# First group of a two-layer decoder trunk: x turned without its row scale, loads on two queues, another order of casts and products

## The chip, the cores and the metric

One core of one Trainium2 chip runs the whole program, the other cores are idle. The metric is the device time of one execution in microseconds (us), as the median of the runs. The engines are named as in the profile: PE (TensorE, matrix products; PEld is its loading of the stationary operand), DVE (VectorE), ACT (ScalarE), POOL (GpSimd), SP (SyncE, which only issues DMA transfers here). ACT can issue DMA transfers too; a row marked SPq or POOLq is such an issue on that engine.

## What is computed

The reference is a trunk of two layers on x of 256 tokens by 1024 features, in float32. Each layer is a SwiGLU block, a mixer (causal pooling in layer 0, dilated attention in layer 1) and a second SwiGLU block, each with an RMS norm ahead of it and one behind it. The change touches only the very first step:

```python
def rms_norm(x, gain):
    y = x * rsqrt(mean(x * x) + eps) * gain

def swiglu(h, w_gate, w_up, w_down):
    return (silu(h @ w_gate) * (h @ w_up)) @ w_down

f = swiglu(rms_norm(x, g[0]), ffn_w_gate[0, 0], ffn_w_up[0, 0], ffn_w_down[0, 0])
```

The factor rsqrt(...) of a row can be applied after the product with the weights, because it is one number per token. The kernel does so: x times the gain goes into the product, and the row factor comes in at the silu and at the product of gate and up.

## The kernel before

Tokens lie in two tiles of 128 rows (i = 0, 1). Every float32 product is made of three products in a shorter format (float32r): each operand is split into a high part (a cast on ACT) and a low part (the original less the high part, on DVE), and PE adds high times high, high times low, low times high. So every block of weights that arrives must pass ACT once and DVE once before PE can use all of it. PE is fed by a stream of weight blocks, `ws`, in the order of their use; a block is 128 x 2048 floats (1 MB), loaded as two halves of 512 KB into one of three buffers `raw` (or two buffers `xy`).

The first group of the first SwiGLU is `opening()` (L635 to L801). It is 512 columns of gate and 512 of up for both token tiles: 8 pieces of weights j = 0 to 7 (gate 0 to 3, up 4 to 7; block b holds pieces 2b and 2b + 1), each used in 6 products for each tile i, which makes 96 products of 128 x 128 by 128 x 512. Pieces 0, 1, 4 and 5 meet the first 512 features of x, pieces 2, 3, 6 and 7 the second 512.

x must be turned (features on partitions) before it can be the stationary operand. For each tile i and half b: `turn_x` (L667) transposes four 128 x 128 pieces on PE; `scaled_x` (L673) multiplies by the gain on DVE; `high_x` (L681) casts on ACT; `low_x` (L684) subtracts on DVE. Ahead of that the kernel before scales each row by the reciprocal of the largest magnitude of its first 128 elements (`size_x`, `rows`, L647 to L660: a reduce, a maximum, a reciprocal and a multiplication on DVE for the first half of a row; a multiplication on ACT for the second), and `q0` puts that size back later. `high(j)` (L687) and `low(j)` (L696) split piece j of the weights; `products(i, j, ...)` (L700) issues the products H (high weights, high x), W (low weights) and X (low x). `keep_warm` (L86) issues small products of zeros while nothing else is there to do.

Inside `manual_schedule` (L708 to L791) the order of the lines is the order of the instructions on PE, DVE, ACT and SP; each of these engines works through its own queue in order and waits at an instruction whose operands are not there. After that block, Tile's scheduler sets the order. What follows: the mean squares of x (`rstd_of`, four squares L203 on ACT, a power on POOL), differences of the turned halves of x (`Sums`, casts L285, subtractions L286), and `pair(1)` (L378), the second group. In it `form` (L124) splits a whole block at once: hl_hi on ACT (L127, 128 x 2048), hl_lo on DVE (L128). The first formed block feeds the 24 products g; a block in buffer xy the 12 products st that follow; then y is added to x on DVE (L376, `add(x, y, 0)`), the sum is formed and used; another block feeds 24 products g; then a third block z is added to x (L376 again), and the sum is formed for the next st products.

Of the kernel before, what the change touches and what calls it, by code (L numbers as in the profile page):

```python
# [11 lines left out]
F32 = mybir.dt.float32  # L12
# [7 lines left out]
P = 128  # L20
# [9 lines left out]
Q_TAIL = 4  # L30
TURN_0, TURN_1 = 3, 0
DMA_SUMS = (2, 3)
WARM = 26
FILL = 9, 5, 8, 4
LEAST = 1e-3
SIZE_OF = 128
EPS = 1e-6
MAGIC = 12582912.0
SIN_MAX = 3.1415925
# [14 lines left out]
def trunk_kernel(ctx: ExitStack, tc: tile.TileContext, x, pos, gains, pscale, ws, wq, invf, amask, pmat, icnt, out):  # L54
# [37 lines left out]
    nc.sync.dma_start(gfirst[0:KC, 0:P], gains[0].rearrange("(k p) -> k p", p=P))  # L92

    block_no = [0]
    last = {}
# [532 lines left out]
            waiting.append(rest)  # L628

    rx = cp.tile([P, 2], F32, name="r_x")  # L630
    q0 = cp.tile([P, 2], F32, name="q_x")
    aT = new_aT("x")
    sums = Sums("x")

    def opening():  # L635


        gcol = cp.tile([P, KC], F32, name="gain_col")
        size = cp.tile([P, 2], F32, name="size_x")
        over = cp.tile([P, 2], F32, name="over_x")  # L640
        raws, highs, units, t, tps = [], [], [], {}, {}
        banks = [accp.tile([P, 512], F32, tag="acc", name=f"acc_b0{k}") for k in range(4)]
        gu = [banks[0::2], banks[1::2]]
        y = [sc4.tile([P, D], F32, tag="y", name=f"n_x{i}") for i in range(2)]
        H, X, W = [(0, 0, 0), (0, 1, 0)], [(1, 0, 0), (1, 1, 0)], [(0, 0, 1), (0, 1, 1)]

        def size_x(i):  # L647
            z = slice(i, i + 1)
            nc.vector.tensor_reduce(
                size[:, z], h[i][:, :SIZE_OF], axis=mybir.AxisListType.X, op=ALU.max, apply_absolute_value=True  # L650
            )
            nc.vector.tensor_scalar(size[:, z], size[:, z], LEAST, None, op0=ALU.max)
            nc.vector.reciprocal(over[:, z], size[:, z])

        def rows(i, b):
            c, z = slice(b * 512, (b + 1) * 512), slice(i, i + 1)
            if b == 0:
                nc.vector.tensor_scalar_mul(y[i][:, c], h[i][:, c], over[:, z])
            else:
                nc.scalar.mul(y[i][:, c], h[i][:, c], over[:, z])  # L660

        def turn_gain():
            tp = tpp.tile([P, 4, P], F32, tag="tp", name="tp_gain")
            nc.tensor.transpose(tp[:, 0, :KC], gfirst[:KC, :P], ident[:KC, :KC])
            nc.scalar.copy(gcol, tp[:, 0, :KC])

        def turn_x(i, b):  # L667
            tps[i, b] = tp = tpp.tile([P, 4, P], F32, tag="tp", name=f"tp_x{i}{b}")
            for c in range(4):
                k = b * 4 + c  # L670
                nc.tensor.transpose(tp[:, c], y[i][:, k * P : (k + 1) * P], ident)

        def scaled_x(i, b):  # L673
            t[i, b] = sums.tmp(f"{i}{b}")
# [6 lines left out]
        def high_x(i, b):  # L681
            nc.scalar.copy(part_of(i, b)[:, 0], t[i, b])
# [3 lines left out]

        def high(j, k=None):  # L687

            if j == len(highs):
                pool, tag = (xyp, "xy") if j < 2 else (hlp, "hl")  # L690
                highs.append(pool.tile([P, 2, 1024], F32R, tag=tag, name="hl"))
                units.append((highs[j][:, 0], highs[j][:, 1]))
            c = slice(0, 1024) if k is None else slice(k * 512, (k + 1) * 512)
            nc.scalar.copy(highs[j][:, 0, c], raws[j // 2][:, j % 2, c])

# [12 lines left out]
        with tc.manual_schedule(  # L708
            engines={
                mybir.EngineType.PE,  # L710
                mybir.EngineType.DVE,
                mybir.EngineType.Activation,
                mybir.EngineType.SP,
            }
        ):
            nc.sync.dma_start(h[1][:, :512], x[P:, :512])
            raw = rawp.tile([P, 2, 1024], F32, tag="raw", name="raw0")
            for k in range(2):
                c = slice(k * 512, (k + 1) * 512)
                nc.sync.dma_start(raw[:, 0, c], ws[0, :, c])  # L720
            raws.append(load_raw(raw=raw, at=1))
            for i in range(2):
                nc.sync.dma_start(h[i][:, 512:], x[i * P : (i + 1) * P, 512:])
            raws.extend(load_raw() for _ in range(2))
            turn_gain()
            keep_warm(FILL[0])
            size_x(0)
            rows(0, 0)
            turn_x(0, 0)
            size_x(1)  # L730
            rows(1, 0)
            scaled_x(0, 0)
            keep_warm(FILL[1])
            turn_x(1, 0)
            scaled_x(1, 0)
            keep_warm(FILL[2])
            high(0, 0)
            high_x(0, 0)
            high(0, 1)
            low(0, 0)  # L740
            products(0, 0, H)
            low_x(0, 0)
            keep_warm(FILL[3])
            high_x(1, 0)
            products(1, 0, H[:1])
            products(0, 0, W[:1], X)
            low(0, 1)
            products(1, 0, H[1:], W[:1])
            products(0, 0, W[1:])
            products(1, 0, W[1:])  # L750
            low_x(1, 0)
            high(1)
            rows(0, 1)
            rows(1, 1)
            low(1)
            products(1, 0, X)
            turn_x(0, 1)
            for i in range(2):
                products(i, 1, H, X)
            turn_x(1, 1)  # L760
            for i in range(2):
                products(i, 1, W)
            high(2)
            scaled_x(0, 1)
            high_x(0, 1)
            scaled_x(1, 1)
            high_x(1, 1)
            low_x(0, 1)
            products(0, 2, H, X)
            low(2)  # L770
            raws.append(load_raw())
            products(1, 2, H)
            high(3)
            low_x(1, 1)
            products(0, 2, W)
            products(1, 2, W, X)
            low(3)
            for i in range(2):
                products(i, 3, H, X)
            for i in range(2):  # L780
                products(i, 3, W)
            for j in range(4, 8):
                high(j)
                low(j)
                if j == 5:
                    for i in range(2):
                        rstd_of(h_halves(i), f"x{i}", rx[:, i : i + 1])
                        nc.gpsimd.tensor_mul(q0[:, i : i + 1], rx[:, i : i + 1], size[:, i : i + 1])
            for i in range(2):
                for j in range(4, 8):  # L790
                    products(i, j, H, X, W)  # L791
        s3 = sums.tmp("s")
        nc.vector.tensor_sub(s3, t[0, 0], t[1, 0])
        sums.parts(2, s3)
# [557 lines left out]
```

## Time and profile before

| what | us |
| --- | --- |
| median of 3 runs | 944.83 (943.65 to 946.33) |
| profiled execution, its own time | 945.04 |
| its span in the trace | 943.3 |
| PE busy in the span | 930.7 |
| DVE busy | 744.8 |
| ACT busy | 565.6 |

In the rows of the timeline the first number is the start in us from the span's start, the second the length; in brackets stands how long the engine was idle ahead of it and what it waited for. In the rows of the chain of waits the same two numbers stand ahead of the engine, the output's name and the line.

### The profile page before, as it was taken

How to read it: one execution, taken by the hardware profiler on the slowest of the kernel's cores; microseconds unless marked ns; L12 is line 12 of the kernel's file. 1: busy time of each engine (PE TensorE's matmuls, PEld its weight loads, DVE VectorE, ACT ScalarE, POOL GpSimd, SP SyncE). 2: the span in 40 equal slices, each digit the busy share in tenths (PEclk: the TensorE clock that was granted, in tenths of full speed). 3: DMA queues.
4: the chain of work that ended last, by engine and by line, in shares of the span. 5: the costliest groups of instructions: out<-in, count | busy, mean ns of one | idle time of the engine just before them, and what ended most of it. 6: DMA issues, size and time to landing. Idle time of an engine off the chain costs nothing.

```text
span 943.3 us, 12011 instructions
## 1 busy us (share of the span) xinstructions
PE 930.7 (99%) x4513; PEld 767.7 (81%) x4513; DVE 744.8 (79%) x822; ACT 565.6 (60%) x692; POOL 42.7 (5%) x66
## 2 busy tenths in 40 slices
PE   9999999999999999999999999999999999999997
PEld 7878888778888888888888888888898778788885
DVE  7888897889877889878888874686287788888964
ACT  6675665556647576567657653554356776576652
POOL 1000000000100000001000000110000010000000
PEclk9999999999999999999999999999999999999999
DMA  8785976765568698675696865375333546969561
GB/s 328 245 261 191 330 250 183 266 227 198 175 197 257 217 296 265 195 252 190 163 335 145 320 238 207 139 237 168 132 101 135 179 167 166 334 135 379 148 209 44
DMA packets 56777, 202.92 MB, mean 215 GB/s; under 512 B 7496, under 2 KB 7504, under 8 KB 53904
## 3 DMA queue, kind: packets, MB, share of 16 engines
q1 hardware_dynamic: 53472, 178.83, 52.9%
q0 software_dynamic: 3248, 23.33, 12.9%
q8 instruction: 35, 0.57, 0.2%
q14 instruction: 22, 0.18, 0.1%
HBM read 178.02 MB, written 1.05 MB: 190 GB/s over the span
## 4 chain that ended last, share of the span: by engine, by line
PE 86%; DVE 5%; ACT 3%; issue 3%; DMA 2%; POOL 0%; SPq 0%; DVEq 0%; POOLq 0%; ACTq 0%
PE st L354 13%; PE g L150 12%; PE acc_d L484 12%; PE acc_b L150 8%; PE u L150 7%; PE acc_d L150 4%; PE qp L150 4%; PE kp L150 3%; PE q L354 3%; PE vp L150 3%; PE acc_w L150 2%; PE acc_d L354 2%; PE acc_u L150 2%; PE htp L333 2%; DMA raw<-in_ws 1%
## 5 line engine op out<-in xcount | busy, mean ns | idle before, releaser
L110 ACT CAST hl<-raw 128x1024 fp32r<-128x1024 f32 x140 | 145.5, 1051 | 96.3 <-PE acc_d L150 21.9
L111 DVE TENSOR_TENSOR hl<-raw,hl 128x1024 fp32r<-128x1024 f32 x140 | 169.3, 1220 | 38.2 <-ACT hl L110 37.1
L128 DVE TENSOR_TENSOR hl_lo<-xy,hl_hi 128x2048 fp32r<-128x2048 f32 x55 | 125.9, 2289 | 62.2 <-ACT hl_hi L127 62.2
L127 ACT CAST hl_hi<-xy 128x2048 fp32r<-128x2048 f32 x55 | 105.2, 1913 | 67.2 <-PE u L150 24.7
L484 PE MATMUL acc_d<-hl,h 128*128 128x512 f32 x576 | 136.8, 392 | 0.0
L128 DVE TENSOR_TENSOR hl_lo<-raw,hl_hi 128x2048 fp32r<-128x2048 f32 x54 | 123.4, 2286 | 15.2 <-ACT hl_hi L127 15.2
L484 PEld LDWEIGHTS acc_d<-hl,h 128*128 128x128 f32 x576 | 107.2, 188 | 23.4 <-DVE acc_d L543 0.9
L127 ACT CAST hl_hi<-raw 128x2048 fp32r<-128x2048 f32 x54 | 103.3, 1913 | 22.9 <-PE st L354 8.9
L335 ACT CAST h<-htp 128x512 fp32r<-128x512 f32 (+1 forms) x48 | 26.4, 550 | 38.0 <-PE htp L333 38.0
L150 PE MATMUL acc_b<-hl,aT_m 128*128 128x512 f32 x192 | 44.9, 392 | 0.7 <-ACT aT_m L243 0.7
L150 PE MATMUL acc_d<-hl,h 128*128 128x512 f32 x192 | 44.6, 392 | 0.0
L150 PEld LDWEIGHTS acc_b<-hl,aT_m 128*128 128x128 f32 x192 | 35.7, 188 | 8.5 <-ACT aT_m L243 1.2
L150 PE MATMUL g<-hl_hi,aT_m 128*128 128x512 f32 x128 | 42.0, 394 | 0.0
L354 PE MATMUL st<-hl_hi,S_m 128*128 128x512 f32 x128 | 41.9, 393 | 0.0
L150 PE MATMUL u<-hl_hi,aT_m 128*128 128x512 f32 x128 | 41.8, 393 | 0.0
L150 PEld LDWEIGHTS acc_d<-hl,h 128*128 128x128 f32 x192 | 35.7, 188 | 7.3
L374 POOL DMA_DIRECT2D xy<-raw x22 | 19.2, 872 | 445.9 <-DVE hl_lo L128 160.6
L150 PE MATMUL qp<-hl,aT_f 128*128 128x384 f32 x192 | 37.3, 343 | 0.0
L150 PE MATMUL kp<-hl,aT_hk 128*128 128x512 f32 x144 | 34.5, 394 | 0.0
L150 PEld LDWEIGHTS qp<-hl,aT_f 128*128 128x128 f32 x192 | 32.9, 188 | 1.3 <-issue 0.9
L336 DVE TENSOR_TENSOR h<-htp,h 128x512 fp32r<-128x512 f32 (+1 forms) x48 | 30.7, 640 | 4.0 <-ACT h L335 3.6
L150 PE MATMUL vp<-hl,aT_hk 128*128 128x512 f32 x144 | 33.1, 390 | 0.0
(316 smaller groups left out, 1848.9 us busy)
## 6 DMA issues: line engine op xcount, KB each, us to landing
raw<-in_ws SPq DMA_DIRECT2D x265, 512.0 KB, 5.1
xy<-in_ws SPq DMA_DIRECT2D x44, 512.0 KB, 7.4
xy<-raw POOLq DMA_DIRECT2D x22, 1024.0 KB, 8.2
rawq<-in_wq SPq DMA_DIRECT2D x8, 768.0 KB, 4.7
gain_post<-in_gains SPq DMA_DIRECT2D x14, 256.0 KB, 7.1
gain_pre<-in_gains SPq DMA_DIRECT2D x10, 256.0 KB, 7.4
h<-in_x SPq DMA_DIRECT2D x4, 256.0 KB, 5.3
rawpm<-in_pmat SPq DMA_DIRECT2D x2, 512.0 KB, 4.6
```

The source lines that it names most:

```text
L110: nc.scalar.copy(hl[:, 0, :n], raw[:, k, :n])
L111: last["dve"] = nc.vector.tensor_sub(hl[:, 1, :n], raw[:, k, :n], hl[:, 0, :n])
L127: nc.scalar.copy(hi, raw)
L128: last["dve"] = nc.vector.tensor_sub(lo, raw, hi)
L150: last["mm"] = nc.tensor.matmul(o, l, r, start=start, stop=stop)
L333: nc.tensor.transpose(tp[:, k], prod[c, i][:, k * P : (k + 1) * P], ident)
L335: nc.scalar.copy(d[:, 0], tp[:, :nt])
L336: nc.vector.tensor_sub(d[:, 1], tp[:, :nt], d[:, 0])
L354: nc.tensor.matmul(ps, a(z, k), u[v], start=start and k == 0 and n == 0, stop=k == 3 and n == 2, skip_group_check=not start,)
L374: nc.gpsimd.dma_start(dst, src, accum_op=ALU.add)
L484: nc.tensor.matmul(f[i][k], d[:, z], u[v][:, r], start=c == 0 and m == 0, stop=m == 2 and (own is not None or c == NF - 1), skip_group_che ...
```

## The change

- `size_x`, `rows`, `size`, `over`, `q0` and the tiles `y` are gone. `turn_x` transposes h, that is x itself; the row factor `rx` is used where `q0` was.
- The gain and the first half of tile 1 of x are loaded from ACT's queue instead of SP's. Piece 0 of the weights (two transfers of 256 KB) stays on SP and follows the first half of tile 0. Piece 1 (512 KB) is issued from ACT, in ACT's order behind the copy of the gain.
- SP then loads block 2 (pieces 4 and 5), the second halves of x, block 1, and later block 3.
- The pieces are split and used in the order 0, 1, 4, 5, 2, 3, 6, 7 instead of 0 to 7. The second halves of x are turned after the products of piece 1 (tile 0) and after the products H and X of piece 4 (tile 1); before, after those of piece 0 and within those of piece 1.
- All eight pieces are cast ahead of the four squares; before, pieces 6 and 7 came behind them.
- `keep_warm` fills: 28, then 14, 2, 2, instead of 26, then 9, 5, 8, 4.

```diff
-WARM = 26
-FILL = 9, 5, 8, 4
+WARM = 28
+FILL = 14, 2, 2
...
-    nc.sync.dma_start(gfirst[0:KC, 0:P], gains[0].rearrange("(k p) -> k p", p=P))
+    nc.scalar.dma_start(gfirst[0:KC, 0:P], gains[0].rearrange("(k p) -> k p", p=P))
...
+        def load(b):
+            raws[b] = rawp.tile([P, 2, 1024], F32, tag="raw", name=f"raw{b}")
+            for k in range(2):
+                last["dma"] = nc.sync.dma_start(raws[b][:, k], ws[b, :, k * 1024 : (k + 1) * 1024])
...
-                nc.tensor.transpose(tp[:, c], y[i][:, k * P : (k + 1) * P], ident)
+                nc.tensor.transpose(tp[:, c], h[i][:, k * P : (k + 1) * P], ident)
...
-            nc.sync.dma_start(h[1][:, :512], x[P:, :512])
+            nc.scalar.dma_start(h[1][:, :512], x[P:, :512])
...
+            turn_gain()
+            nc.scalar.dma_start(flat[:, 1024:], ws[0, :, 1024:2048])
+            load(2)
             for i in range(2):
                 nc.sync.dma_start(h[i][:, 512:], x[i * P : (i + 1) * P, 512:])
+            load(1)
             turn_x(0, 0)
...
+            load(3)
+            turn_x(0, 1)
+            scaled_x(0, 1)
+            high_x(0, 1)
+            high(5)
+            low_x(0, 1)
+            low(5)
+            for i in range(2):
+                products(i, 4, H, X)
             turn_x(1, 1)
...
-    ffn(0, aT, sums, go, q=q0)
+    ffn(0, aT, sums, go, q=rx)
```

What this makes of the order of the instructions is shown at three places. The first is the front of ACT's queue. raw_174 and raw_171 are the buffer of pieces 0 and 1, raw_180 that of pieces 2 and 3 in the kernel before, raw_178 that of pieces 4 and 5 in the changed one; tp_gain is the turned gain, aT_x the turned x, sum_x x times the gain. The kernel before:

```order
L665 COPY gain_col<-tp_gain 128x8
L694 CAST hl<-raw_174 128x512
L682 CAST aT_x<-sum_x_211 128x4x128
L694 CAST hl<-raw_174 128x512
L682 CAST aT_x<-sum_x_223 128x4x128
L694 CAST hl<-raw_174 128x1024
L660 ACTIVATE n_x_169<-h_100,over_x 128x512
L660 ACTIVATE n_x_170<-h_101,over_x 128x512
L694 CAST hl<-raw_180 128x1024
L682 CAST aT_x<-sum_x_287 128x4x128
L682 CAST aT_x<-sum_x_290 128x4x128
```

The same place in the changed kernel:

```order
L649 COPY gain_col<-tp_gain 128x8
L705 DMA raw_171<-in_ws 128x1024
L677 CAST hl<-raw_171 128x512
L666 CAST aT_x<-sum_x_191 128x4x128
L666 CAST aT_x<-sum_x_198 128x4x128
L677 CAST hl<-raw_171 128x512
L677 CAST hl<-raw_171 128x1024
L677 CAST hl<-raw_178 128x1024
L666 CAST aT_x<-sum_x_265 128x4x128
L677 CAST hl<-raw_178 128x1024
L666 CAST aT_x<-sum_x_289 128x4x128
```

A DMA issue now stands ahead of the first cast. It waits for a semaphore: the semaphores of the transfers are used in turn, and the one of this transfer is that of the first transfer of piece 0, which must have landed. The casts of the second halves of x (the last aT_x rows) stand behind casts of pieces 4 and 5.

The second place is ACT's queue from the last casts of the opening to the first formed block. jk_x are the squares, S_x the casts of the differences, s the silu, raw_428 and raw_405 the first formed block. The kernel before:

```order
L203 ACTIVATE jk_x_333,ss_x_332<-h_100 128x512
L203 ACTIVATE jk_x_335,ss_x_332<-h_100 128x512
L203 ACTIVATE jk_x_342,ss_x_341<-h_101 128x512
L203 ACTIVATE jk_x_344,ss_x_341<-h_101 128x512
L694 CAST hl<-raw_299 128x1024 x2
L285 CAST S_x<-sum_xs 128x512
L285 CAST S_x<-sum_x_223 128x512
L285 CAST S_x<-sum_x_211 128x512
L317 ACT_TABLE_LOAD
L317 ACTIVATE s_0_418<-acc_b_165,q_x 128x512
L127 CAST hl_hi<-raw_428 128x2048
```

The changed kernel:

```order
L677 CAST hl<-raw_257 128x1024 x2
L201 ACTIVATE jk_x_318,ss_x_317<-h_100 128x512
L283 CAST S_x<-sum_xs 128x512
L201 ACTIVATE jk_x_320,ss_x_317<-h_100 128x512
L283 CAST S_x<-sum_x_198 128x512
L201 ACTIVATE jk_x_326,ss_x_325<-h_101 128x512
L315 ACT_TABLE_LOAD
L315 ACTIVATE s_0_395<-acc_b_164,r_x 128x512
L201 ACTIVATE jk_x_328,ss_x_325<-h_101 128x512
L283 CAST S_x<-sum_x_191 128x512
L125 CAST hl_hi<-raw_405 128x2048
```

The same instructions stand ahead of the first formed block: two casts of the last pieces, four squares, three casts of differences, the table load and one silu. Only their order among themselves is another.

The third place is DVE's queue from the first formed block to the second add. xy_466 and xy_443 are the buffer x of `pair(1)`, h the turned result of the first group, m the product of gate and up. The kernel before:

```order
L128 TENSOR_TENSOR hl_lo<-raw_428,hl_hi 128x2048
L286 TENSOR_TENSOR S_x<-sum_x_287,S_x 128x512
L128 TENSOR_TENSOR hl_lo<-xy_466,hl_hi 128x2048
L325 SCALAR_TENSOR_TENSOR m_0_424<-acc_b_168,q_x,s_0_422 128x512
L376 TENSOR_TENSOR xy_466<-xy_466,xy_469 128x2048
L336 TENSOR_TENSOR h_0_0_155<-htp_00_447,h_0_0_155 128x4x128
L128 TENSOR_TENSOR hl_lo<-xy_466,hl_hi 128x2048
L128 TENSOR_TENSOR hl_lo<-raw_521,hl_hi 128x2048
L336 TENSOR_TENSOR h_0_0_155<-htp_01_491,h_0_0_155 128x4x128
L376 TENSOR_TENSOR xy_466<-xy_466,raw_498 128x2048
```

The changed kernel:

```order
L126 TENSOR_TENSOR hl_lo<-raw_405,hl_hi 128x2048
L284 TENSOR_TENSOR S_x<-sum_x_265,S_x 128x512
L323 SCALAR_TENSOR_TENSOR m_0_401<-acc_b_167,r_x,s_0_399 128x512
L126 TENSOR_TENSOR hl_lo<-xy_443,hl_hi 128x2048
L334 TENSOR_TENSOR h_0_0_156<-htp_00_424,h_0_0_156 128x4x128
L374 TENSOR_TENSOR xy_443<-xy_443,xy_446 128x2048
L126 TENSOR_TENSOR hl_lo<-xy_443,hl_hi 128x2048
L334 TENSOR_TENSOR h_0_0_156<-htp_01_468,h_0_0_156 128x4x128
L126 TENSOR_TENSOR hl_lo<-raw_498,hl_hi 128x2048
L374 TENSOR_TENSOR xy_443<-xy_443,raw_475 128x2048
```

These are the same ten instructions. The first h row, which needs transposes by PE and a copy by ACT, has moved from behind the first add to ahead of it.

More of the change, by code (lines that the diff above doesn't have):

```diff
@@ L687, in high @@
         def high(j, k=None):
[L689 removed]
+            if j not in highs:
                 pool, tag = (xyp, "xy") if j < 2 else (hlp, "hl")
[L691 to L692 removed]
+                highs[j] = pool.tile([P, 2, 1024], F32R, tag=tag, name="hl")
             c = slice(0, 1024) if k is None else slice(k * 512, (k + 1) * 512)
@@ L715, in opening @@
         ):
-            nc.sync.dma_start(h[1][:, :512], x[P:, :512])
[L717 to L721, printed above, removed]
+            nc.scalar.dma_start(h[1][:, :512], x[P:, :512])
+            raws[0] = rawp.tile([P, 2, 1024], F32, tag="raw", name="raw0")
+            flat = raws[0].rearrange("p k n -> p (k n)")
@@ L722, in opening @@
+            for c in (slice(0, 512), slice(512, 1024)):
+                nc.sync.dma_start(flat[:, c], ws[0, :, c])
+            turn_gain()
+            nc.scalar.dma_start(flat[:, 1024:], ws[0, :, 1024:2048])
+            load(2)
             for i in range(2):
                 nc.sync.dma_start(h[i][:, 512:], x[i * P : (i + 1) * P, 512:])
[L724 to L728, printed above, removed]
+            load(1)
@@ L729, in opening @@
             turn_x(0, 0)
-            size_x(1)
-            rows(1, 0)
             scaled_x(0, 0)
-            keep_warm(FILL[1])
             turn_x(1, 0)
             scaled_x(1, 0)
-            keep_warm(FILL[2])
+            keep_warm(FILL[0])
             high(0, 0)
             high_x(0, 0)
-            high(0, 1)
[L740 to L746, printed above, removed]
@@ L747, in opening @@
-            low(0, 1)
-            products(1, 0, H[1:], W[:1])
+            low(0, 0)
+            low_x(0, 0)
+            products(0, 0, H[:1])
+            keep_warm(FILL[1])
+            high_x(1, 0)
+            products(0, 0, W[:1])
+            products(1, 0, H[:1], W[:1])
+            products(0, 0, X[:1])
+            keep_warm(FILL[2])
+            high(0, 1)
+            low_x(1, 0)
+            low(0, 1)
+            products(0, 0, H[1:])
+            products(1, 0, H[1:])
+            high(1)
@@ L749, in opening @@
+            products(0, 0, X[1:])
+            products(1, 0, X)
+            low(1)
             products(0, 0, W[1:])
             products(1, 0, W[1:])
[L751 to L757, printed above, removed]
+            high(4)
+            low(4)
             for i in range(2):
                 products(i, 1, H, X)
+            for i in range(2):
+                products(i, 1, W)
@@ L760, in opening @@
+            load(3)
[5 more added lines that the diff above has]
+            low(5)
+            for i in range(2):
+                products(i, 4, H, X)
             turn_x(1, 1)
             for i in range(2):
[L762 to L765, printed above, removed]
+                products(i, 4, W)
             scaled_x(1, 1)
             high_x(1, 1)
-            low_x(0, 1)
@@ L769, in opening @@
[L769 to L773, printed above, removed]
-            low_x(1, 1)
[L775 to L782, printed above, removed]
+            low_x(1, 1)
+            for j in (2, 3, 6, 7):
                 high(j)
@@ L784, in opening @@
                 low(j)
[L785 to L788, printed above, removed]
             for i in range(2):
-                for j in range(4, 8):
+                products(i, 5, H, X, W)
+            for i in range(2):
+                rstd_of(h_halves(i), f"x{i}", rx[:, i : i + 1])
+            for i in range(2):
+                for j in (2, 3):
@@ L791, in opening @@
                     products(i, j, H, X, W)
+            for i in range(2):
+                for j in (6, 7):
+                    products(i, j, H, X, W)
+            block_no[0] = 4
         s3 = sums.tmp("s")
```

23 lines of the change are left out of this document (2 added, 21 removed).

## The prediction

> **What bounds the kernel now.** I first read the busy times of the page and then the chain of waits over the first 60 us, because the change touches only the first group.
>
> ```profile
> span 943.3 us, 12011 instructions
> PE 930.7 (99%) x4513; PEld 767.7 (81%) x4513; DVE 744.8 (79%) x822; ACT 565.6 (60%) x692; POOL 42.7 (5%) x66
> ```
>
> PE is busy for 99% of the span, so a microsecond by which PE's queue is later at 60 us is a microsecond at the end, and one that it gains there is gained at the end. What decides when PE gets to 60 us is another question. The chain of waits from 14 to 50 us, in order of time:
>
> ```profile
> 14.43 0.70 DVE sum_x L676
> 15.15 0.62 ACT aT_x L682
> 15.77 2.85 ACT hl L694 x3
> 18.62 0.63 ACT jk_x L203 x2
> ...
> 26.97 1.81 ACT hl_hi L127
> ...
> 28.80 1.13 DVE hl_lo L128
> ...
> 43.98 2.21 DVE xy L376
> ...
> 48.02 1.92 ACT hl_hi L127
> 49.98 0.49 PE st L354
> ```
>
> There is no PE in it between 14.43 and 49.98. The path starts at the turned second half of x (aT_x), goes through everything that ACT has queued up to the first formed block, and on through DVE and ACT until PE waits for them at 50 us. PE's waits there:
>
> ```profile
> 49.98 0.19 PEld L354 LDWEIGHTS st<-hl_hi,S_x 128*128 128x128 f32 x1 [0.67 <-ACT hl_hi L127]
> 50.50 0.19 PEld L354 LDWEIGHTS st<-hl_lo,S_x 128*128 128x128 f32 x1 [0.33 <-DVE hl_lo L128]
> ```
>
> So up to 50 us the cover that PE's products give to ACT and DVE is used up. If ACT and DVE get there later, PE stops for the difference; if only PE gets there earlier, it waits longer. I therefore follow ACT's queue, and PE only where ACT waits for it.
>
> **The change part by part.** The start of the opening on ACT, DVE, PE and SP:
>
> ```profile
> 0.74 0.39 SPq L74 DMA_DIRECT2D h<-in_x  x1
> 1.19 0.36 SPq L92 DMA_DIRECT2D gain_first<-in_gains  x1
> 2.01 0.90 SPq L720 DMA_DIRECT2D raw<-in_ws  x2
> 2.95 0.43 SPq L102 DMA_DIRECT2D raw<-in_ws  x1
> 3.58 0.28 DVE L649 TENSOR_REDUCE size_x<-h 128x1 f32<-128x128 f32 x1 [2.65 <-DMA h<-in_x]
> 6.19 0.62 ACT L694 CAST hl<-raw 128x512 fp32r<-128x512 f32 x1 [1.84 <-DMA raw<-in_ws]
> 7.38 0.62 ACT L682 CAST aT_x<-sum_x 128x512 fp32r<-128x512 f32 x1 [0.57 <-DVE sum_x L676]
> 8.05 1.02 PE L150 MATMUL acc_b<-hl,aT_x 128*128 128x512 f32 x2
> 9.14 1.05 ACT L694 CAST hl<-raw 128x1024 fp32r<-128x1024 f32 x1
> ```
>
> *No row scale, first weights sooner.* The steps of the scale on DVE go, and with them the 0.57 us for which the cast of x waited at 7.38. But the first weights are there only at 6.19 (the cast waited for that DMA). In the changed kernel their transfer is SP's second instead of its fourth, so it is issued about where the gain's is now, at 1.19 instead of 2.01. The same bytes are ahead of it. It lands between 5.4 (all of those 0.8 us) and 6.2 (nothing, if bytes decide); I take 5.7.
>
> *The first product.* ACT now issues the transfer of piece 1 between that landing and the first cast. SP's issue of the same size took 0.43 us (2.95); ACT's isn't shown and I take the same. Then come a cast of weights (0.62) and a cast of x (0.62), so the first product is at 5.7 + 0.43 + 2 x 0.62 = 7.4 instead of 8.05: 0.65 us sooner, with both bounds 7.1 and 7.9.
>
> *Piece 1.* It was issued at 2.95 and was there for the cast at 9.14. Now it is issued at 5.7. How long it takes from there:
>
> ```profile
> DMA to landing us min/median/max: 4.2/6.9/9.2
> ...
> raw<-in_ws SPq DMA_DIRECT2D x265, 512.0 KB, 5.1
> ```
>
> The first row is for the weights of the first 30 us, the second for all of them. A transfer with nothing ahead of it took 2.84 us (x's first, issued at 0.74, used at 3.58; 256 KB). ACT's queue has nothing ahead of piece 1, but SP's transfers run beside it. The bounds are 2.8 and 6.9; I take 4.4, near the quickest of the opening, because it waits behind none of its own queue. Piece 1 lands at 10.1 and its cast ends at 11.15. PE by then:
>
> ```profile
> 16.91 14.87 PEld L150 LDWEIGHTS acc_b<-hl,aT_x 128*128 128x128 f32 x66 [0.37 <-DVE hl L698]
> 13.95 0.45 PE tp_x L671 x4
> ```
>
> A product takes 14.87 / 66 = 0.225 us. The 12 products of piece 0 take 2.7 us and some short waits from 7.4 on, until 10.2. PE waits about 0.9 us for piece 1, to 11.15.
>
> On the two queues the Trainium skill, page DMA: Bandwidth & Descriptors, section Issuing engines are not separate DMA queues, says that transfers of all issuing engines run on the same 16 DMA engines and interleave, and that several issuers save only the time of issuing. What it would make of the time is the second rival below.
>
> *The second halves of x.* In the kernel before their casts are at
>
> ```profile
> 13.06 0.62 ACT L682 CAST aT_x<-sum_x 128x512 fp32r<-128x512 f32 x1
> 15.15 0.62 ACT L682 CAST aT_x<-sum_x 128x512 fp32r<-128x512 f32 x1 [1.47 <-DVE sum_x L676]
> 17.37 3.49 DVE L698 TENSOR_TENSOR hl<-raw,hl 128x1024 fp32r<-128x1024 f32 x3
> ```
>
> Now PE turns tile 0 only behind the 12 products of piece 1: 11.15 + 2.7 + 0.45 = 14.3. DVE scales it (0.7), ACT casts it at 15.2 to 15.8 and then piece 5 (2.85 / 3 = 0.95) to 16.8. DVE takes the low part of piece 5 (3.49 / 3 = 1.16) to 18.0, then scales the half of tile 1 (0.7), which PE turned meanwhile, and ACT casts it at 18.75 instead of 15.15. The last half of x is 3.6 us later on ACT. ACT's waits ahead of these two casts (from 12.1, when piece 4 is cast, to 15.2, and from 16.8 to 18.75) have no cover, since ACT is the path.
>
> *From there to the first formed block.* Before, from 15.15 to the start of hl_hi:
>
> ```profile
> 26.86 1.90 ACT L127 CAST hl_hi<-raw 128x2048 fp32r<-128x2048 f32 x1
> 28.80 2.29 DVE L128 TENSOR_TENSOR hl_lo<-raw,hl_hi 128x2048 fp32r<-128x2048 f32 x1 [0.39 <-ACT hl_hi L127]
> 36.77 0.68 DVE L336 TENSOR_TENSOR h<-htp,h 128x512 fp32r<-128x512 f32 x1
> ```
>
> That is 11.71 us, with five casts of pieces, four squares, three casts S_x, the table load and one silu. Afterwards it is the same list with four casts of pieces instead of five, since 4 and 5 are done and 2 has moved behind: 11.71 - 0.95 = 10.76. That the squares come last changes nothing in this sum, because all of them still stand ahead of hl_hi on ACT. It starts at 18.75 + 10.76 = 29.5 instead of 26.86: 2.65 us later. The two multiplications by the row scale that ACT loses lay ahead of 15.15, where ACT waited anyway.
>
> *From hl_hi to 50 us.* DVE has the same ten instructions to the second add. Before, the h row (0.68) lay at 36.77, in the time in which DVE waited for ACT's hl_hi at 36.94. Now it is ahead of the add, so 0.7 us of cover is lost, and it waits for PE's transposes besides, which come behind 12 products (2.7 us) that start when hl_lo of the first block is there; DVE has 3.5 us of other work in that time (S_x, m and the low part of x: 0.6, 0.7 and 2.2), so this wait is short. I take 1.0 for both, with 0.7 and 1.2 as bounds. After 60 us the order of all engines is that of before, and PE has no further term.
>
> **The sum**: 2.65 + 1.0 = 3.65 us on the profiled execution of 945.04 (its span of 943.3 and 1.7 around it), hence 948.7. That execution took 0.2 us more than the median of the runs, which is left in. By the bounds: with first weights at 5.4 and piece 1 in 2.8 us, PE doesn't wait for it and begins it 1.25 us sooner, 2.4 us in all, 947.4. With 6.2 and the 5.1 of the whole program it is 0.5 + 0.7 more, 949.9.
>
> **The rivals.**
>
> *First: PE alone decides.* If ACT and DVE catch up, what counts is PE's own queue: 0.65 us earlier, nothing lost in pieces 2 to 7, hence 944.4, and no slower than before. For it: PE is busy at 99%, and ACT only at 60%. Its place is the first formed block: DVE's hl_lo ended at 28.80 + 2.29 = 31.1, and the loads of the 96 products end at 16.91 + 14.87 = 31.8, so 0.7 us were free. It decides if hl_hi starts by about 27 in the changed kernel. Against it: the chain above has no PE in it, and the list on ACT has hardly become shorter while its start moves from 15.15 to 18.75.
>
> *Second: the queues share.* The transfers run at a rate that the DMA engines set (the last two columns are their busy share and GB/s, from 2 to 3 us and from 8 to 32):
>
> ```profile
> 2.00:3.00 1.00, 1.00 (x13) 1.00 (x11) 0.00 (x0) 0.02 (x1) 0.00 (x0) 1.00 0.79 244
> ...
> 8.00:32.00 24.00, 23.93 (x108) 18.91 (x109) 21.61 (x29) 21.42 (x30) 1.89 (x4) 1.00 0.96 366
> ```
>
> At a DMA share of 0.96 and 366 GB/s a second queue adds nothing: the first weights still come at 6.2, and piece 1 gets half: 0.524 MB at 183 GB/s is 2.9 us, and with the 2.1 us that the first transfer of x took beside its bytes (2.84 less 0.262 MB at 366 GB/s) it takes 5.0. That is 0.5 + 0.6 on the sum, 949.8. The interleaving that the Trainium skill states (the page named above) is this case. For it: the share. Against it: from 2 to 3 us the share was only 0.79, so transfers issued earlier can use what was free there.
>
> *Third: piece 1 comes late.* With the 6.9 us that is the median of the opening, everything behind it moves by 2.5: 951.2. For it: most transfers of the opening took that. Against it: those waited behind others of their own queue.
>
> **How the numbers follow.** The forecast has 0.55, the second rival 0.12, the third 0.10, the first 0.20, since a schedule made by hand from the rows of another kernel can miss; 0.03 is left for a gain larger than any that I can derive. A measurement of this kernel can tell 0.3%, 2.8 us, from no change, so slower begins at 947.7. Of the forecast a fifth lies below it: slower is 0.44 + 0.12 + 0.10 = 0.66, same 0.11 + 0.20 = 0.31, faster 0.03. The likeliest time is 948.7, its own range 947.4 to 949.9. To hold 8 in 10 the range takes in the first rival and the second and leaves out the third and the rest: 944.3 to 950.6.
>
> **What would show it.** Right: the cast of the last half of x on ACT at 18 to 19 us, hl_hi of the first formed block at 29 to 30, PE waiting 1 to 2 us for its hl_lo and again for the blocks of the st products before 60 us, and none after. A wait of about 1 us of ACT and PE for piece 1 near 10 us. Wrong: hl_hi at 27 or sooner, or PE without waits between 30 and 60 us. Then the first rival holds. A first product at 7.9 or later with piece 1 at 11 speaks for the second.

## The result and the profile after

| | before | changed |
| --- | --- | --- |
| median, us | 945.29 (943.65 to 946.33, 4 runs) | 950.81 (950.05 to 952.24, 4 runs) |
| profiled execution | 945.04, span 943.3 | 952.24, span 950.5 |

The ratio is 1.0063, with a 95% interval of 1.0050 to 1.0076: the change costs 5.5 us, where 3.65 were forecast. The profiled execution of the changed kernel is the slowest of its four, so its trace is used for where the time lies and the medians for how much it is.

The busy times of the page:

```profile
span 950.5 us, 11984 instructions
PE 931.1 (98%) x4507; PEld 767.2 (81%) x4507; DVE 743.1 (78%) x814; ACT 563.8 (59%) x690; POOL 43.5 (5%) x64
```

PE has as much to do as before (931.1 us beside 930.7), so the time is waiting. The chain of waits of the changed kernel over the first 80 us, start and length in us:

```profile
1.19 3.96 DMA raw<-in_ws
5.17 7.13 DMA raw<-in_ws
...
12.33 1.05 ACT hl L677
...
13.43 3.06 PE acc_b L148 x12
16.49 0.45 PE tp_x L655 x4
...
17.69 0.62 ACT aT_x L666
...
27.80 2.07 POOL r_x L209
...
31.71 1.82 ACT hl_hi L125
...
33.55 2.30 DVE hl_lo L126
...
40.17 2.29 DVE xy L374
...
53.81 2.30 DVE hl_lo L126
...
56.16 5.55 PE st L352 x23
61.71 5.44 PE u L148 x24
```

The second row is piece 1: 7.13 us on the path, from its issue on ACT's queue until its landing. Only from 56 us on is the chain PE's alone. The rows of ACT's timeline with the casts that the prediction names:

```profile
5.17 0.34 ACTq L705 DMA_DIRECT2D raw<-in_ws  x1
5.55 0.62 ACT L677 CAST hl<-raw 128x512 fp32r<-128x512 f32 x1 [0.98 <-DMA raw<-in_ws]
...
12.33 1.99 ACT L677 CAST hl<-raw 128x1024 fp32r<-128x1024 f32 x2 [3.93 <-DMA raw<-in_ws]
17.69 0.62 ACT L666 CAST aT_x<-sum_x 128x512 fp32r<-128x512 f32 x1 [3.37 <-DVE sum_x L660]
...
21.15 0.62 ACT L666 CAST aT_x<-sum_x 128x512 fp32r<-128x512 f32 x1 [1.89 <-DVE sum_x L660]
...
31.61 1.91 ACT L125 CAST hl_hi<-raw 128x2048 fp32r<-128x2048 f32 x1
```

ACT stands idle for 3.93 us until piece 1 is there. The last half of x is cast at 21.15 instead of 15.15, and the first formed block starts at 31.61 instead of 26.86. The loads of stationary operands for which PE then waits:

```profile
35.90 0.19 PEld L148 LDWEIGHTS g<-hl_lo,aT_x 128*128 128x128 f32 x1 [1.37 <-DVE hl_lo L126]
46.77 0.19 PEld L352 LDWEIGHTS st<-hl_lo,S_x 128*128 128x128 f32 x1 [2.02 <-DVE hl_lo L126]
56.16 0.19 PEld L352 LDWEIGHTS st<-hl_lo,S_x 128*128 128x128 f32 x1 [1.35 <-DVE hl_lo L126]
```

and the start of the products u, from which on both kernels are fed in the same way:

```profile
61.55 0.39 PE L148 MATMUL u<-hl_hi,aT_x 128*128 128x512 f32 x1
```

The same row of the kernel before:

```profile
55.66 0.39 PE L150 MATMUL u<-hl_hi,aT_x 128*128 128x512 f32 x1
```

Two numbers carry what follows: **F**, the start of the first formed block's hl_hi on ACT, and **U**, the start of the u products on PE. F is what the opening makes, U - F what DVE and ACT make of the next 29 us.

### The profile page after: what moved, and what is told of

It is laid out like the page before. It is cut to its first block, busy times and chain, and to the rows that moved or that the text cites. A ratio compares the mean times of both kernels' runs of the same rounds, so it can differ in the third digit from the quotient of the medians.

```text
span 950.5 us, 11984 instructions
## 1 busy us (share of the span) xinstructions
PE 931.1 (98%) x4507; PEld 767.2 (81%) x4507; DVE 743.1 (78%) x814; ACT 563.8 (59%) x690; POOL 43.5 (5%) x64
## 3 DMA queue, kind: packets, MB, share of 16 engines
HBM read 178.02 MB, written 1.05 MB: 188 GB/s over the span
## 4 chain that ended last, share of the span: by engine, by line
PE 83%; DVE 7%; issue 3%; DMA 3%; ACT 3%; POOL 0%; SPq 0%; DVEq 0%; POOLq 0%; ACTq 0%
PE st L352 12%; PE acc_d L482 12%; PE g L148 12%; PE u L148 7%; PE acc_b L148 6%; PE acc_d L148 5%; PE qp L148 4%; PE kp L148 3%; PE q L352 3%; PE vp L148 3%; PE acc_w L148 2%; PE acc_d L352 2%; PE acc_u L148 2%; DMA raw<-in_ws 2%; PE htp L331 2%
```

## The experiments

The theory, called A: piece 1 takes 7 us because SP's outstanding transfers share the DMA engines with it; ACT's list, and F with it, move by that; the h row ahead of the add on DVE makes U - F longer; the total is U and a constant. The rivals differ from run to run and stand in what was expected.

The table gives the results. "Piece 1" is from its issue to the start of its cast, which waited for the DMA (with "<": the cast didn't wait, so it is a bound). The last column is the profiled execution's time less U.

| kernel | median, us (range, runs) | ratio to before, interval | piece 1 | F | U | U - F | rest |
| --- | --- | --- | --- | --- | --- | --- | --- |
| before | | | <6.2 | 26.86 | 55.66 | 28.80 | 889.4 |
| changed | 950.81 (950.05 to 952.24, 4) | 1.0063 [1.0050, 1.0076] | 7.2 | 31.61 | 61.55 | 29.94 | 890.7 |
| g3, changed again | 951.31 (949.86 to 953.33, 6) | 1.0069 [1.0051, 1.0087] | 6.7 | 30.82 | 60.71 | 29.89 | 889.2 |
| e1 | 948.74 (947.85 to 949.80, 5) | 1.0042 [1.0027, 1.0056] | <6.9 | 29.98 | 59.92 | 29.94 | 888.8 |
| e2 | 948.49 (947.43 to 951.08, 6) | 1.0041 [1.0026, 1.0055] | 7.5 | 28.53 | 58.43 | 29.90 | 889.0 |
| e3 | 946.63 (945.53 to 947.58, 11) | 1.0020 [1.0010, 1.0029] | <6.1 | 27.08 | 57.18 | 30.10 | 888.7 |
| e4 | 944.08 (943.14 to 948.76, 12) | 0.9997 [0.9985, 1.0009] | <7.4 | 29.58 | 58.38 | 28.80 | 890.4 |
| f1 | 950.59 (949.40 to 953.21, 6) | 1.0059 [1.0047, 1.0071] | 7.4 | 31.06 | 60.03 | 28.97 | 890.7 |
| g4, f1 again | 950.63 (948.24 to 952.53, 6) | 1.0055 [1.0035, 1.0076] | 7.8 | 33.68 | 62.67 | 28.99 | 888.8 |
| f2 | 948.76 (948.20 to 949.19, 5) | 1.0037 [1.0025, 1.0049] | 7.8 | 30.80 | 59.60 | 28.80 | 888.6 |
| f3 | 945.85 (944.99 to 947.59, 11) | 1.0007 [0.9999, 1.0016] | | 27.29 | 57.03 | 29.74 | 889.1 |
| f4 | 943.94 (942.52 to 945.94, 11) | 0.9987 [0.9979, 0.9996] | | 24.09 | 54.87 | 30.78 | 891.1 |
| g1 | 951.27 (949.76 to 953.06, 4) | 1.0067 [1.0047, 1.0087] | 7.2 | 30.94 | 60.84 | 29.90 | 888.9 |
| g2 | 950.03 (948.64 to 950.17, 4) | 1.0050 [1.0032, 1.0068] | 6.2 | 29.81 | 59.71 | 29.90 | 890.3 |

Each group had its own runs of the kernel before, and the ratio is to those: 944.22 for e1 to e4, 945.58 for f1 to f4, 944.71 for g1 to g4. g5 was run once (954.89) and is told with g1 and g2. The rest lies between 888.6 and 891.1 without an order in it, so one profiled execution says U to a tenth and the total only to about 1.2 us.

**e1: piece 1 on SP, straight behind piece 0.**

```diff
+            nc.sync.dma_start(flat[:, 1024:], ws[0, :, 1024:2048])
             turn_gain()
-            nc.scalar.dma_start(flat[:, 1024:], ws[0, :, 1024:2048])
```

> The changed kernel with piece 1 issued on SP straight behind piece 0, and so off ACT; all other orders as in the changed kernel. Theory A (the path is ACT's and DVE's list; late are the start of piece 1, the turned second halves of x and the h row ahead of the add): piece 1 lands at about 9, PE goes from piece 0 to piece 1 without a wait of more than 0.5 us, hl_hi of the first formed block starts at about 28.5 instead of 31.6, and 3 us come back: 947.5 to 948.3, still 2 to 3 us above the kernel before. Rival R1 (the late piece 1 is the whole loss): 945 to 945.5, with hl_hi at 27 or sooner. Rival R2 (the transfers share, no matter who issues them): 950 or more, piece 1 still at 11 or later.

948.74, 2.1 less than the changed kernel, and F 1.6 sooner, where A had 947.5 to 948.3 and F 3 us sooner. It lies between R1 and R2. ACT's timeline in e1:

```profile
8.32 1.65 ACT L677 CAST hl<-raw 128x512 fp32r<-128x512 f32 x2
10.20 1.05 ACT L677 CAST hl<-raw 128x1024 fp32r<-128x1024 f32 x1 [0.22 <-DMA raw<-in_ws]
16.06 0.62 ACT L666 CAST aT_x<-sum_x 128x512 fp32r<-128x512 f32 x1 [4.81 <-DVE sum_x L660]
```

The second cast of the first row is that of piece 1, and it waits for nothing. What is late next is PE: ACT waits 4.81 us for the turned x, which stands behind 24 products on PE. So the late piece is worth about 2 us, perhaps more: PE itself began late in this execution (the second four transposes took 1.11 us instead of the 0.66 of the changed kernel, the first product stood at 8.29 instead of 7.08), as it did in g3's trace, with the granted clock at 1.00 in both; why is open. Whether the rest of the loss lies in the turning order is what e3 asks.

**e2: piece 1 on ACT, but issued at 1.76, ahead of the table load.**

```diff
             nc.scalar.dma_start(h[1][:, :512], x[P:, :512])
             raws[0] = rawp.tile([P, 2, 1024], F32, tag="raw", name="raw0")
             flat = raws[0].rearrange("p k n -> p (k n)")
+            nc.scalar.dma_start(flat[:, 1024:], ws[0, :, 1024:2048])
...
             turn_gain()
-            nc.scalar.dma_start(flat[:, 1024:], ws[0, :, 1024:2048])
```

> The changed kernel with piece 1 still issued on ACT, but at once, behind the first half of tile 1 of x and ahead of the table load, without the wait for piece 0. If the late issue made piece 1 late: it lands at 8 to 9.5, the time comes to 947.5 to 948.5, like with SP. If sharing with SP's transfers made it late: it lands at 10.5 or later, the time stays at 949 to 951. In both cases the first weights may come later than the 5.5 us of the changed kernel, up to 6.5, since three transfers run beside each other.

948.49, F 28.53. The issue and the cast that waits for it, in ACT's timeline of e2:

```profile
1.76 0.44 ACTq L702 DMA_DIRECT2D raw<-in_ws  x1
...
9.22 2.00 ACT L677 CAST hl<-raw 128x1024 fp32r<-128x1024 f32 x2 [0.50 <-DMA raw<-in_ws]
```

Issued 3.4 us sooner it is there 3.1 us sooner, and F moves by 3.1. It takes 7.5 us here too: what is bought is the earlier issue, not a shorter transfer. By what was expected, the late issue made piece 1 late (it lands at 9.2, within 8 to 9.5). That it still takes 7.5 us is taken up behind g5.

**e3: e1, and the second halves of x turned where the kernel before turns them.**

```diff
             high(4)
-            low(4)
+            turn_x(0, 1)
             for i in range(2):
                 products(i, 1, H, X)
+            turn_x(1, 1)
...
```

> As the kernel with piece 1 on SP, and the second halves of x turned behind piece 0 and within piece 1, as in the kernel before. Theory A: the cast of the last half of x on ACT goes from about 18 to 13 to 15.5, hl_hi starts at 25.5 to 27, DVE's h row is behind the add again, and the time is 944.5 to 945.8, the kernel before's within 0.8 us. Rival R1 (the order of the turns is beside the point): no change against the kernel with piece 1 on SP, 947.5 to 948.3 or what that one measured. Risk: the second halves of x land only behind block 2, and PE may wait for them until 11 or 12.

946.63: 2.1 less than e1, F 2.9 sooner, near that of before. So the turning order is worth about as much as the late piece. The time is above A's range (944.5 to 945.8): what e3 still has above before is 2.4 us (0.2%, interval 0.1 to 0.3%), of which the trace shows 1.5 in U, 1.3 of it in U - F. The h row, which A blamed for that, is behind the add again in e3; f3 below shows what else does it.

**e4: the kernel before without the row scale, nothing else.**

```diff
-                nc.tensor.transpose(tp[:, c], y[i][:, k * P : (k + 1) * P], ident)
+                nc.tensor.transpose(tp[:, c], h[i][:, k * P : (k + 1) * P], ident)
...
-    ffn(0, aT, sums, go, q=q0)
+    ffn(0, aT, sums, go, q=rx)
```

> The kernel before without the row scale alone (x turned as it is, the row factor rx in the place of q0); loads and orders as before. Theory A: the chain starts at the cast of the last half of x, which waits for PE and for the landing of block 1 at about 12, so only the 0.5 us by which PE starts sooner can come through: 944.5 to 945.3. Rival (PE's own queue decides): the first product at 7.4 instead of 8.05 comes through in full, 944.3 to 944.8. If the scale was a cost on the path beyond that: 944 or less.

944.08, no difference from before. Its profiled execution is the slowest of the 12, so its F of 29.58 is not typical. The unscaled x by itself makes no difference that these runs can tell (interval -0.15 to +0.09%, about a microsecond either way).

**f1 and g4: the add of x and y ahead of the h row on DVE.**

```diff
+            if (n, c, i) == (0, 0, 0):
+                last["h_row"] = lambda: nc.vector.tensor_sub(d[:, 1], tp[:, :nt], d[:, 0])
+                return
...
-                nc.vector.tensor_add(dst, dst, src)
+                last["add"] = nc.vector.tensor_add(dst, dst, src)
...
+            if "h_row" in last:
+                with in_turn("add"):
+                    last.pop("h_row")()
```

> The changed kernel, but VectorE does the first add of x and y ahead of its row on h instead of behind it, as in the kernel before. Theory A (the time is the start of the first formed block, F, plus the stretch from there to the u products, and the h row ahead of the add is what makes that stretch 29.94 instead of 28.80 us): F stays at about 31.6, the stretch falls to about 28.9, 949.6 to 950.0 us, 1.0 less than the changed kernel. Rival B (the stretch is longer because of the scaled squares' rows and the pow on GpSimd, which takes 2.06 instead of 0.86 us; the order on VectorE doesn't matter): stretch 29.9, 950.5 to 951.1.

> The changed kernel with the add of x and y ahead of the row on h, a second time, on the same chip as the changed kernel itself. Theory A (the row costs the chain 1 us): 0.7 to 1.3 us less than the changed kernel beside it, the stretch from F to the u products again near 28.9. Rival B (what is gained there is lost again behind 60 us): within 0.4 of the changed kernel, with longer waits of PE behind 60 us.

> The changed kernel once more, for the run that follows and for the spread of piece 1's landing. Theory A: 950.0 to 951.2, piece 1 lands 6.5 to 7.5 us after its issue. Rival (7.1 us was one late execution, the usual one is near 5): piece 1 near 10, F near 29.5.

DVE's timeline in f1:

```profile
36.48 2.28 DVE L126 TENSOR_TENSOR hl_lo<-xy,hl_hi 128x2048 fp32r<-128x2048 f32 x1
38.80 2.29 DVE L377 TENSOR_TENSOR xy<-xy,xy 128x2048 f32<-128x2048 f32 x1
41.01 0.68 DVE L335 TENSOR_TENSOR h<-htp,h 128x512 fp32r<-128x512 f32 x1
```

The add directly follows hl_lo, and U - F is 28.97 and 28.99 with this order, and 29.94, 29.89, 29.90 and 29.90 in the four kernels that differ from these only in loads or not at all (the changed kernel, g3, g1, g2). By the traces the order of the row and the add is worth 0.95 us, as A has it, with the pow and the squares left as they were. The medians don't show it: 950.59 and 950.63, beside 950.81 and 951.31. That is 0.2 and 0.7 less with ranges of 4 us, and 950.59 lies in B's range and not in A's, so the total is left inconclusive. g3 also shows that the late piece 1 wasn't one odd execution: 6.7 us.

**f2: the kernel before with the changed loads alone** (gain, half of x and piece 1 from ACT).

```diff
-            nc.sync.dma_start(h[1][:, :512], x[P:, :512])
+            nc.scalar.dma_start(h[1][:, :512], x[P:, :512])
...
             turn_gain()
+            nc.scalar.dma_start(raw[:, 1], ws[0, :, 1024:2048])
```

> The kernel before with nothing of the change but the loads: gain and half of x on ScalarE's queue, the second quarter of the first weights on ScalarE's queue behind the gain copy. Theory A (that quarter takes 7 us from its issue whenever SyncE's transfers run beside it, and PE and ScalarE's list wait for it): first weights at 5.2 to 5.5, the quarter at 11 to 12.5, F 1.5 to 2.5 us later than before's 26.86, 946.2 to 947.5. Rival B (the lateness comes from the turned order and what waits in it, the loads alone cost nothing): F 26.5 to 27.2, 944.0 to 945.0.

948.76, 3.2 more than before, above A's range and far from the rival's. ACT's timeline in f2:

```profile
4.28 0.34 ACTq L727 DMA_DIRECT2D raw<-in_ws  x1
4.65 0.62 ACT L694 CAST hl<-raw 128x512 fp32r<-128x512 f32 x1 [0.30 <-issue]
...
12.09 1.04 ACT L694 CAST hl<-raw 128x1024 fp32r<-128x1024 f32 x1 [2.91 <-DMA raw<-in_ws]
```

The first weights are cast 1.5 us sooner than before, and piece 1 2.95 us later (9.14 to 12.09). Without any other order of turning the loads alone cost more than half of the change's 5.5 us. That it is more than A's 2.5 probably has to do with the clock, which takes 1.6 us in f2's trace (last section).

**f3: the kernel before with the four squares behind the casts of pieces 6 and 7.**

```diff
-                if j == 5:
-                    for i in range(2):
-                        rstd_of(h_halves(i), f"x{i}", rx[:, i : i + 1])
-                        nc.gpsimd.tensor_mul(q0[:, i : i + 1], rx[:, i : i + 1], size[:, i : i + 1])
+            for i in range(2):
+                rstd_of(h_halves(i), f"x{i}", rx[:, i : i + 1])
+                nc.gpsimd.tensor_mul(q0[:, i : i + 1], rx[:, i : i + 1], size[:, i : i + 1])
```

> The kernel before with the four squares of x behind the casts of the sixth and seventh quarter of the weights instead of between them. The prediction's claim (the casts wait for landings there, and the squares fill the wait wherever they stand): no change, 944.0 to 945.0. Rival (behind the last cast the squares stand on ScalarE's list right ahead of the first formed block, four times 0.6 us less the 1.5 us of waiting that they no longer fill): F up to 0.9 us later, 945.0 to 945.9.

945.85, 0.3 us above the 945.58 of before beside it, with an interval that holds zero (-0.1 to +1.5 us); it lies in the rival's range. In its trace F is 0.43 later, and U 1.37. The other 0.94 is on DVE, in f3's timeline:

```profile
29.75 1.29 DVE L286 TENSOR_TENSOR S_x<-sum_x,S_x 128x512 fp32r<-128x512 f32 x2 [0.29 <-ACT S_x L285]
30.96 2.28 DVE L128 TENSOR_TENSOR hl_lo<-raw,hl_hi 128x2048 fp32r<-128x2048 f32 x1
...
36.03 2.28 DVE L376 TENSOR_TENSOR xy<-xy,xy 128x2048 f32<-128x2048 f32 x1
```

With the squares last, two rows S_x come between the end of hl_hi (29.21) and the first hl_lo, where the kernel before has one behind it, and the add starts 8.74 us behind F instead of 7.71 (34.57 - 26.86). In five traces U - F goes with that stretch from F to the add: 7.71 and 28.80 in the kernel before, 7.74 and 28.97 in f1, 8.56 and 29.94 in the changed kernel, 8.74 and 29.74 in f3, 8.88 and 30.10 in e3. In f3 and e3 the h row is behind the add. So it isn't that row alone: by these traces what counts is how much DVE does between F and the add.

**g1, g2 and g5: what runs beside piece 1.** g1 takes pieces 2 and 3 (1.05 MB) away from beside it, g2 the second halves of x as well (0.52 MB more), g5 also pieces 4 and 5. ACT issues them later instead. Here is g2; g5 has `load(2, nc.scalar)` ahead of these lines and all of them behind the cast of piece 1, so that its time (954.89, one run, beside 944.06) tells nothing.

```diff
-            for i in range(2):
-                nc.sync.dma_start(h[i][:, 512:], x[i * P : (i + 1) * P, 512:])
-            load(1)
...
             high(0, 1)
+            for i in range(2):
+                nc.scalar.dma_start(h[i][:, 512:], x[i * P : (i + 1) * P, 512:])
+            load(1, nc.scalar)
```

> The changed kernel, but the 1 MB of pieces 2 and 3 isn't issued on SyncE from 4.25 us on, beside piece 1; ScalarE issues it behind its second cast, near 8.5. Theory A (piece 1 takes 7.1 us from its issue because the other queue's outstanding transfers share the DMA engines with it; from 5.17 to 12.3 us these moved 2.6 MB, of which about 0.4 MB was pieces 2 and 3): piece 1 lands about 1.2 us sooner, near 11.1; 949.2 to 950.2. Rival (a transfer issued by ScalarE takes about 7 us whatever runs beside it): 12.0 to 12.5, 950.2 to 951.2.

> As the run before, and the second halves of x (0.5 MB) are held back to the same place, so that beside piece 1 there are only piece 0, pieces 4 and 5 and the first halves of x. Piece 1 is issued about 1 us sooner than in the changed kernel, near 4.3, since it no longer takes the place of the first weights' transfer among those that an issue waits for. Theory A (sharing): it takes 4.5 to 5.5 us, lands at 8.8 to 9.8, the start of the first formed block F moves from 31.6 to 28.6 to 29.6, 947.6 to 949.0. Rival (7 us whatever runs beside it): 11.3, 949.5 to 950.3.

> One look, for piece 1's landing alone: of the changed kernel's transfers only piece 0 and the first halves of x are issued ahead of piece 1's cast; pieces 2 to 5 and the second halves of x are issued by ScalarE behind that cast, so that everything behind it is late by design. When piece 1 is issued, near 4.4, 1.05 MB have been issued and about 0.65 MB of that moved: 0.4 MB are outstanding, 0.92 with piece 1. Theory A (a transfer takes as long as the engines need for all bytes that are outstanding, at about 370 GB/s, and 1 to 2 us more): it lands 3.0 to 4.5 us after its issue. Rival (ScalarE's queue, or the size alone, makes it 6 to 7 us): at 10.4 or later. The time, 952 to 957, decides nothing.

ACT's timelines, first g1, then g2, then g5 (each the issue and the cast):

```profile
4.41 0.33 ACTq L705 DMA_DIRECT2D raw<-in_ws  x1
...
11.66 2.00 ACT L677 CAST hl<-raw 128x1024 fp32r<-128x1024 f32 x2 [3.29 <-DMA raw<-in_ws]
```

```profile
4.38 0.33 ACTq L705 DMA_DIRECT2D raw<-in_ws  x1
...
10.55 2.00 ACT L677 CAST hl<-raw 128x1024 fp32r<-128x1024 f32 x2 [2.42 <-DMA raw<-in_ws]
```

```profile
4.41 0.33 ACTq L705 DMA_DIRECT2D raw<-in_ws  x1
...
8.20 1.05 ACT L677 CAST hl<-raw 128x1024 fp32r<-128x1024 f32 x1 [0.16 <-DMA raw<-in_ws]
```

7.2, 6.2 and 3.8 us. By its duration g1 speaks for the rival, and its 951.27 is that of the changed kernel beside it (g3, 951.31); g2's landing lies between the two (10.55, where A had 9.8 at most and the rival 11.3), and its 950.03 lies in the rival's range. g5 decides: the same transfer from the same queue takes 3.8 us when almost nothing runs beside it. The bytes say why g1 and g2 gave so little. The rates ahead of the issue and from the issue to the cast (the last two columns are the DMA engines' busy share and GB/s), in the changed kernel, g2 and g5:

```profile
0.00:5.17 5.17, 4.18 (x33) 3.79 (x33) 0.11 (x1) 1.45 (x2) 0.73 (x7) 1.00 0.60 183
5.17:12.30 7.13, 4.91 (x35) 3.50 (x34) 3.79 (x6) 2.30 (x4) 0.00 (x0) 1.00 1.02 370
```

```profile
0.00:4.38 4.38, 3.38 (x30) 3.17 (x31) 0.11 (x1) 1.28 (x2) 0.73 (x7) 1.00 0.52 155
4.38:10.55 6.17, 5.35 (x38) 3.81 (x38) 3.79 (x6) 2.54 (x5) 0.00 (x0) 1.00 1.01 386
```

```profile
0.00:4.41 4.41, 3.42 (x30) 3.20 (x31) 0.11 (x1) 1.29 (x2) 0.74 (x7) 1.00 0.51 175
4.41:8.04 3.63, 3.56 (x27) 2.64 (x28) 2.52 (x5) 2.54 (x5) 0.00 (x0) 1.00 0.63 222
```

In the changed kernel 3.15 MB had been issued when piece 1 was (the first halves of x, piece 0, pieces 4 and 5, the second halves of x, piece 2), and 183 x 5.17 = 0.95 MB had moved. With piece 1's 0.52 that leaves 2.7 MB, and until it landed 370 x 7.13 = 2.64 MB moved. In g2 it is 2.10 - 0.68 + 0.52 = 1.9 MB left and 2.4 moved, so about 0.4 of that must be of what ACT issued from 7.0 on behind it. In g5 it is 1.05 - 0.77 + 0.52 = 0.8 left and 0.8 moved, at 222 GB/s. So in these three piece 1 lands about when the engines have moved all that was outstanding at its issue, whichever queue that came from, and something of what is issued behind it. In e2 that something is large: at 1.76 only 1.6 MB had been issued, piece 1 included, and none of it moved; until 9.22 the engines moved 317 x 7.46 = 2.4 MB, 0.8 of it issued later. What is outstanding at the issue is thus an estimate that can come out far too low, not a law. In g1 the held-back megabyte came at 7.24, early enough to share the end.

**f4: a candidate.** The kernel before with x unscaled, gain and half of x on ACT, piece 1 left on SP, and both second halves of x turned directly behind the first products.

```diff
-            nc.sync.dma_start(h[1][:, :512], x[P:, :512])
+            nc.scalar.dma_start(h[1][:, :512], x[P:, :512])
...
+            turn_x(1, 1)
...
```

> The kernel before with x unscaled, gain and half of x on ScalarE's queue, and both second halves of x turned directly behind the first products; the quarter of the weights stays on SyncE. Theory A (SyncE's queue carries the weights in order, so nothing is late; the cast of the last half of x is about 1.6 us sooner, but the list of ScalarE then ends on landings of the last raw block near 25.9, and VectorE's rows of the sums that were moved behind the first formed block cost up to 1.3 us): 943.2 to 944.8. Rival (the sooner turn alone carries through): 942.7 to 943.2.

943.94 beside 945.58, inside A's range: 0.13% faster than before, interval 0.04 to 0.21%, the only version of these that is faster than both kernels by more than the noise. In its trace, which is of the slowest of its eleven executions, F is 2.8 us sooner, and U only 0.8. PE's loads in f4 have one wait left between 28 and 62 us:

```profile
49.52 0.19 PEld L352 LDWEIGHTS st<-hl_lo,S_x 128*128 128x128 f32 x1 [1.39 <-DVE hl_lo L126]
```

From 28 us to U only about 1.4 us can still be gained: here PE's own queue decides, as in the prediction's first rival.

## Why the prediction was wrong

- *The bound.* Right. In the changed kernel the chain up to 56 us holds two transfers, ACT, DVE, one row of POOL and little PE, and what F and U lost came out at the end: from the changed kernel to e1, e2, e3 and f2 the medians move with U to about 0.8 us. f4 shows the limit: with F at 24.09 PE decides.
- *First weights and first product.* Right in kind, more than taken: landed at 5.15 (5.7 forecast, the bound was 5.4), first product at 7.08 (7.4). The issue on ACT took 0.34 (0.43).
- *Piece 1: the step that failed.* "I take 4.4, near the quickest of the opening, because it waits behind none of its own queue": 7.1 was measured, past the upper bound of 6.9, and 6.7 to 7.8 in the other runs that issue it at the same place, beside the same transfers (f1, g3, g4) or the other order of them (f2). It landed at 12.30 instead of 10.1, PE waited for it 2.6 us instead of 0.9. The reason given was wrong: the bytes outstanding ahead of it, most of them SP's, count too, 2.2 of the 2.7 MB that were left at its issue. (ACT's own queue wasn't quite empty either: PE waited until 5.84 for the half of tile 1 of x, 0.26 MB.) With 0.3 MB left beside its own it takes 3.8 (g5). The stated range didn't hold the step's own doubt either: its upper end, 949.9, was worked out with 5.1 us; with the bound of 6.9 the same sum gives 945.04 + 3.65 + 0.5 + 2.5 = 951.7.
- *The second halves of x, and the list up to hl_hi.* Right in size once piece 1 is set. From the cast of piece 1 to F the forecast had 29.5 - 10.1 = 19.4 us, the trace has 31.61 - 12.33 = 19.3. The last half of x is cast at 21.15 (18.75), hl_hi starts at 31.61 (29.5): both later by what piece 1 was later. The prediction put the squares' place at nothing; in f3's trace it moves F by 0.4.
- *From hl_hi to 50 us.* Right: U - F is 1.14 longer in the trace, 1.0 was taken. The traces of f1 and g4 give 0.95 of that to the h row; their medians leave it open.
- *The sum.* 3.65 with piece 1 at 10.1; with 12.3 it is 3.65 + 2.2 = 5.85, and U came 5.89 later. The medians differ by 5.5.
- *The rivals.* The first didn't hold, except in f4. The second had the mechanism, and the Trainium skill (page DMA: Bandwidth & Descriptors, section Issuing engines are not separate DMA queues) states it: transfers of all issuers interleave on the same engines. The traces agree, 3.8 us nearly alone (g5) and 7.1 beside SP's transfers. But its price of 5.0 us shared the rate between two queues, while piece 1 got 0.524 of the 2.64 MB moved, a fifth. The third, 6.9 us and 951.2, came closest in size. What was said against it, that the slow transfers waited behind others of their own queue, is what failed.

## What to carry to other kernels

Price a transfer by what is outstanding on all queues at its issue, its own bytes included, over the rate that the trace shows (here 2.7 MB at 370 GB/s, 7.3 us), and not by whether its own queue is empty. That can come out too low: by the same sum g5 comes to 2.2 us and took 3.8, and e2, with more issued behind it, to 4.2 and took 7.5. On a second queue an early issue is worth its time (e2), a late one is a late landing. When a chain is worked out row by row, an unknown near its start moves everything behind it one to one, so that one deserves the widest bounds.

## What was not expected of the hardware

**Behind a short wait of PE its clock can be halved for 3.4 us.** In g4 PE waited 2.91 us for piece 1. The 12 products behind that wait, in PE's timeline:

```profile
13.92 4.23 PE L148 MATMUL acc_b<-hl,aT_x 128*128 128x512 f32 x12 [2.91 <-ACT hl L683]
```

They took 4.23 us instead of the 3.06 of the changed kernel's profiled execution, where PE had waited 2.58. The granted clock (third column from the right) in g4:

```profile
14.00:15.00 1.00, 1.00 (x5) 0.82 (x6) 1.00 (x1) 0.82 (x1) 0.00 (x0) 1.00 0.98 401
15.00:16.00 1.00, 1.00 (x5) 0.82 (x4) 1.00 (x2) 0.00 (x0) 0.00 (x0) 0.71 0.21 82
16.00:17.00 1.00, 1.00 (x4) 0.80 (x3) 0.26 (x1) 0.00 (x0) 0.00 (x0) 0.50 0.71 193
17.00:18.00 1.00, 1.00 (x4) 0.61 (x3) 0.00 (x0) 0.00 (x0) 0.00 (x0) 0.50 0.94 225
18.00:19.00 1.00, 1.00 (x6) 1.00 (x5) 0.00 (x0) 0.00 (x0) 0.00 (x0) 0.58 1.05 410
```

At a clock of 0.50 for the missing part, 0.71 is 0.58 of a microsecond and 0.58 is 0.84: with the two full ones 3.4 us. From the cast of piece 1 to F it is 20.9 us instead of 19.3. f2's trace has the same between 14 and 18 us, behind a wait of 2.0 us: eight products take 3.66 us there where the changed kernel's eight take 2.10, 1.6 us that A hadn't counted. e4's profiled execution, the slowest of its 12, has it between 11 and 15 us, behind a wait of 2.0. The Trainium skill (page TensorE: Matmul & The Clock Gate, section Part 1: The HAM clock gate) has a free-running window of about 3.4 us after which an idle PE gets half its clock; the length agrees, and the waits here were shorter than one window. That the wait causes the drop isn't shown: behind 2.58 us in the changed kernel and 2.67 in f1 there was none. g3's six times fall into 949.9 to 950.3 and 952.3 to 953.3; the mean granted clock was 0.998 to 0.999 in the shorter three and 0.995 to 0.997 in the longer three, and half the clock for 3.4 of 950 us takes 0.002 off a mean. That fits, but only one of the shorter ones was traced. In f2 the mean was 0.996 or 0.997 in all five executions, so the drop in its trace is probably the usual case there.

**The pow on POOL takes 0.86 us in the kernel before and 2.06 in the changed one**, with the same operands, and lies in the chain there (the row at 27.80). It followed 26.5 us without work on POOL instead of 19.8; what makes the difference is open. ACT's table load was over at 29.75 and its silu, which waits for the pow, started at 29.90, so the longer pow cost at most about 0.15 us.
